# Wider margins for the state-loop products, the merging steps and the chunk-map steps of a hybrid decoder layer

## The chip, the cores and the metric

One core of a Trainium2 chip runs the kernel. The metric is the device time of one execution in microseconds (us); lower is better. The times below are the runs of the kernel before and one profiled execution of it.

## The reference

One decoder layer on 512 tokens of width 2048, all in float32: RMSNorm, one input projection, three groups of heads, a gate, an output projection and the residual. Cut to what matters here:

```python
h = _rms(x, norm_g)
proj = h @ w_in                                   # (512, 2048) @ (2048, 7296)
pa, pb, pc = _split(proj, (A_COLS, B_COLS, C_COLS))
r, k, v, ga, wd, ad = _split(_token_shift(pa, mu_a), ...)
ya = _rwkv7(r, k, v, wd, ad, ...) * silu(ga)      # 12 heads of 64: the delta rule
yb = _pool(pu, pool_w, pool_scale) * silu(pg)     # trailing means
yc = _stick_breaking(qc, kc, vc, ...) * silu(gc)  # 12 heads of causal attention
x = x + concatenate([ya, yb, yc]) @ w_out

# _rwkv7, for each token of each head:
sa = einsum('vk,k->v', state, -kk_t)
state = state * w_t + outer(sa, kk_t * a_t) + outer(v_t, k_t)
y_t = einsum('vk,k->v', state, r_t)
```

## The kernel before, in words

**The projections.** The input projection is cut into 57 tiles of 128 columns. Three of them are computed at the start, the other 54 one after the other (`project`, line 482). A tile takes 16 blocks of 128 rows in two half tiles of 8 blocks; each block takes three matmuls of 512 columns (`three`, line 454), because each operand is held as a rounded high part and a low rest (`hh`, `hl`; `wh`, `wl`). So a half tile is 24 matmuls. Its 512 KB of weights come by a transfer on SP's queue into `raw`; ScalarE makes `wh`, VectorE makes `wl` (`split_weights`, line 445), one half tile ahead. The output projection (`oacc`, from line 1074) follows in the same manner, in four column blocks; the first block goes through the 16 row blocks of y in the list `Y_ORDER`, 12 matmuls for each. In that list the last pair of the delta rule stands at place 14 (from 0).

**The delta rule** (`rwkv`, line 554) runs for six pairs of heads, each as a chunked form with 8 chunks of 64 tokens. For a pair: products for decay and rates; products between keys in a chunk (`gm`, into `lt`, `amr`, `bx`); transfers out and back; an inversion of 32 x 32 blocks as 30 dependent pairs of VectorE operations (`pr`, `xblk`); transfers back into `lt`; then the **merging** of the blocks (`xt`, 32 matmuls `q1` from line 710, a copy `w1`, 32 matmuls `q2` from line 720); the **chunk maps** (16 matmuls `am` from line 736, copied by ScalarE to `amx`, then in two halves 16 matmuls `gh` each from line 744, which VectorE adds into `bx`); and the **state loop** (line 776): for each of 8 chunks one product `s` with the state, whose two halves VectorE scales into the next chunk's place in `uv`, and one product `y`. At the end the output is normalised (`mu`, `var`, line 796 on) and gated (`y<-yc,y`, line 810).

**What may start when.** A pair's first work waits until the inversion of the pair before is done (line 557), and its `bk` and `amr` until the pair before has its chunk maps (`done[("mid", p)]`, line 753). Its state loop waits for the state loop before.

**Who sets the order.** Side work (delta rule, attention, pooling) is written as generators. After each matmul of a projection `pump` (line 417) lets every generator go on whose time has come. That time is worked out while the program is written, from a clock `pace` that adds up assumed costs of matmuls and of the other engines' operations (lines 98 to 190). A generator yields a function made by `need` or `need2`: the assumed time at which its inputs are ready and a PSUM bank is free, plus a margin. So the margin says how many matmuls of the projection are written into TensorE's order ahead of the step; on the chip TensorE takes its instructions in that order and waits if the inputs are late. The general margin `MARGIN` is 2.5; two shorter ones serve the delta rule's serial parts:

```python
def need(*tiles, tag=None, margin=MARGIN):                                   # line 388
        return margin + (max(t, pace.bank_at(tag, BANKS[tag])) if tag else t)

yield need(xt, tag="g", margin=QUICK)                                        # line 707, merging, ahead of q1
yield need(w1, tag="g", margin=QUICK)                                        # line 718, merging, ahead of q2
yield need(lt, amt, tag="c", margin=QUICK)                                   # line 734, am, two halves
yield need2(amx, bx, tag="c", margin=QUICK)                                  # line 742, gh, two halves
yield need(bx, uv, tag="y" if cc % 4 == 0 else None if last else "c", margin=TIGHT)   # line 778, each of 8 chunks
```

If an output-projection row block is asked for and its generator is not through, `load_y` (line 1039) pumps all generators at once, without matmuls between (`pump(True)`). VectorE's evictions of `q1`, `q2`, `gh` and `s` stand in blocks `with urgent()`, which move them forward in their engine's order.

Of the kernel before, what the change touches and what calls it, by code (L numbers as in the profile page):

```python
# [51 lines left out]
NFIRST = 3  # L52
BANKS = {"pj": 2, "g": 3, "c": 2, "y": 1}
MARGIN = 2.5
TIGHT = 0.8
AHEAD = 300
EVACUATE = 25
DL = 4.0
QUICK = 1.0
SCAN = 150  # L60
TP = 16

# [155 lines left out]
def hybrid_trunk_kernel(ctx: ExitStack, tc: tile.TileContext, x, xT, w_in, w_out, vecs, consts, up_w, pool_w, out):  # L218
# [41 lines left out]
    def gb(s="g"):  # L260
        return bank("g", s)

    def cb(s="c"):
        return bank("c", s)
# [123 lines left out]
    def need(*tiles, tag=None, margin=MARGIN):  # L388
        def at():
            t = max([pace.ready.get(Pace.key(a), 0.0) for a in tiles] + [0.0])  # L390
            return margin + (max(t, pace.bank_at(tag, BANKS[tag])) if tag else t)

        return at

    def need2(*tiles, tag="g", margin=MARGIN):
        def at():
            q = pace.slots.get(tag, [])
            t = max([pace.ready.get(Pace.key(a), 0.0) for a in tiles] + [0.0])
            free = sorted([pace.read.get(k, 1e9) for k in q] + [0.0] * (BANKS[tag] - len(q)))
            return margin + max(t, free[1])  # L400

        return at
# [151 lines left out]
    def rwkv(p):  # L554
# [149 lines left out]
        with urgent():  # L704
            for h in range(2):
                dve.transpose(xt3[h * HD:h * HD + B], lt[h * HD:h * HD + B, :, h, 0:B])
        yield need(xt, tag="g", margin=QUICK)
        q1 = gb("q1")
# [5 lines left out]
        with urgent():  # L714
            for h in range(2):
                r0 = h * HD + B
                dve.tensor_copy(out=w1[r0:r0 + B, :], in_=q1[r0:r0 + B, :NC_ * B])
        yield need(w1, tag="g", margin=QUICK)
        q2 = gb("q2")
# [13 lines left out]
        for half in range(2):  # L733
            yield need(lt, amt, tag="c", margin=QUICK)
            g = cb("am")
# [4 lines left out]
        for half in range(2):  # L740
            cs = slice(4 * half, 4 * half + 4)
            yield need2(amx, bx, tag="c", margin=QUICK)
            gs = [cb("gh"), cb("gh")]
# [32 lines left out]
        for cc in range(NC_):  # L776
            last = cc + 1 == NC_
            yield need(bx, uv, tag="y" if cc % 4 == 0 else None if last else "c", margin=TIGHT)
            if not last:
# [384 lines left out]
```

## Time and profile before

| | us |
|---|---|
| runs of the kernel, median (lowest to highest, 3 runs) | 1031.54 (1031.24 to 1035.27) |
| the profiled execution's own time | 1034.42 |
| its span in the profile | 1032.6 |

| engine | busy us | share of the span | instructions |
|---|---|---|---|
| TensorE matmul (PE) | 989.5 | 96% | 5132 |
| TensorE weight load (PEld) | 791.3 | 77% | 5132 |
| VectorE (DVE) | 660.9 | 64% | 1249 |
| ScalarE (ACT) | 512.0 | 50% | 838 |
| GpSimd (POOL) | 151.8 | 15% | 204 |

In the rows, a start is in us from the start of the span. "128*128 128x512" is a matmul's stationary and moving operand. Matmuls overlap: a row may say 0.39 us where the next one starts 0.23 us later. What stands in square brackets, or after the second bar of a group, is idle time of the engine just before, with what ended it. Line L380 is the helper of all matmuls, L212 of all work on the other engines, so groups are told apart by their tiles: `s<-uv,bx` writes `s` and reads `uv` and `bx`. The tiles `q1` and `q2` stand there as `q`.

### The profile page before, as it was taken

The page shows a single profiled execution, that of the slowest core. Times are in us where ns is not written, and L with a number is a line of the kernel's source. Part 1 is how long each engine was busy: PE and PEld are TensorE (multiplying, and loading weights), DVE is VectorE, ACT ScalarE, POOL GpSimd, SP SyncE. Part 2 cuts the span into 40 slices and gives each one's busy share as a digit, 9 for nine tenths or more (in the row PEclk, how much of TensorE's full clock was granted, in tenths as well). Part 3 has the DMA queues.
Part 4 walks back from the last instruction along what each step waited for, and adds up shares of the span by engine and source line. Part 5 has one row for each costly group of instructions (what it writes and reads, how often), then busy time and mean ns, then how long its engine had stood idle before and what let it go on. Part 6 is the DMA issues. An engine that isn't in the chain of part 4 may idle for free.

```text
span 1032.6 us, 13786 instructions
## 1 busy us (share of the span) xinstructions
PE 989.5 (96%) x5132; PEld 791.3 (77%) x5132; DVE 660.9 (64%) x1249; ACT 512.0 (50%) x838; POOL 151.8 (15%) x204
## 2 busy tenths in 40 slices
PE   8999989899899999999998998999999999999998
PEld 7868876787677786778777776777877888888886
DVE  5369674868749686697857778478884666323132
ACT  5656654656456555647546464355663345122211
POOL 0122211021211212102110021111221111000000
PEclk9999999999999999999999999999999999999999
DMA  9522232122221323113231222312232237724241
GB/s 340 199 87 84 90 93 97 52 77 97 88 82 62 90 83 109 71 61 95 84 117 43 86 68 96 103 59 76 92 95 95 74 136 257 262 88 139 102 143 61
DMA packets 62211, 109.18 MB, mean 106 GB/s; under 512 B 29760, under 2 KB 31168, under 8 KB 62144
## 3 DMA queue, kind: packets, MB, share of 16 engines
q1 hardware_dynamic: 62144, 108.30, 31.3%
q8 instruction: 40, 0.66, 0.3%
q14 instruction: 27, 0.22, 0.1%
HBM read 98.84 MB, written 9.44 MB: 105 GB/s over the span
## 4 chain that ended last, share of the span: by engine, by line
PE 39%; DVE 29%; issue 15%; ACT 8%; POOL 5%; DMA 2%; SPq 0%; POOLq 0%; DVEq 0%
PE oacc L380 17%; PE pj L380 16%; DVE wl L212 5%; DVE xblk L212 3%; DVE pr L212 3%; DVE n L212 3%; DVE bx L212 3%; POOL e L212 2%; ACT e L212 2%; PE first L380 2%; ACT n L212 2%; DVE u L212 1%; DVE amr L212 1%; DVE w L212 1%; ACT wh L212 1%
## 5 line engine op out<-in xcount | busy, mean ns | idle before, releaser
L380 PE MATMUL pj<-hh,wl 128*128 128x512 f32 x864 | 346.2, 401 | 14.0 <-DVE wl L212 14.0
L380 PE MATMUL pj<-hh,wh 128*128 128x512 f32 x864 | 345.8, 400 | 2.6 <-ACT wh L212 2.4
L380 PE MATMUL pj<-hl,wh 128*128 128x512 f32 x864 | 346.1, 401 | 0.0
L212 DVE TENSOR_TENSOR wl<-raw,wh 128x1024 fp32r<-128x1024 f32 x140 | 175.9, 1257 | 158.4 <-ACT wh L212 157.9
L212 ACT CAST wh<-raw 128x1024 fp32r<-128x1024 f32 x140 | 146.5, 1047 | 201.3 <-PE oacc L380 118.0
L380 PEld LDWEIGHTS pj<-hh,wl 128*128 128x128 f32 x864 | 163.9, 190 | 53.8 <-DVE wl L212 20.1
L380 PEld LDWEIGHTS pj<-hh,wh 128*128 128x128 f32 x864 | 163.9, 190 | 37.4 <-ACT wh L212 4.1
L380 PEld LDWEIGHTS pj<-hl,wh 128*128 128x128 f32 x864 | 164.0, 190 | 34.5 <-issue 2.2
L380 PE MATMUL oacc<-wl,yh 128*128 128x512 f32 x256 | 100.0, 391 | 0.0
L380 PE MATMUL oacc<-wh,yh 128*128 128x512 f32 x256 | 99.6, 389 | 0.0
L380 PE MATMUL oacc<-wh,yl 128*128 128x512 f32 x256 | 99.6, 389 | 0.0
L212 POOL TENSOR_SCALAR e<-e 128x512 f32<-128x512 f32 x28 | 45.0, 1607 | 200.1 <-ACT e L212 183.9
L212 DVE TENSOR_TENSOR_SCAN n<-n,m 128x512 f32<-128x512 f32 (+3 forms) x48 | 40.9, 866 | 32.7 <-ACT n L212 32.7
L212 POOL TENSOR_TENSOR d<-u 128x512 f32<-128x512 f32 x25 | 39.4, 1577 | 146.9 <-DVE u L212 90.1
L380 PEld LDWEIGHTS oacc<-wh,yl 128*128 128x128 f32 x256 | 48.0, 188 | 10.1 <-issue 0.2
L380 PEld LDWEIGHTS oacc<-wl,yh 128*128 128x128 f32 x256 | 48.0, 188 | 10.1 <-issue 0.2
L380 PEld LDWEIGHTS oacc<-wh,yh 128*128 128x128 f32 x256 | 48.0, 188 | 10.1
L212 ACT ACTIVATE e<-e 128x512 f32<-128x512 f32 x50 | 31.5, 630 | 33.4 <-POOL e L212 33.1
L212 DVE TENSOR_TENSOR u<-pj,rstd 128x512 f32<-128x512 f32 x50 | 34.3, 686 | 20.9 <-PE pj L380 20.6
L212 POOL CAST kl<-klo 64x512 fp32r<-64x512 f32 x24 | 20.9, 869 | 168.9 <-DVE klo L212 124.1
L212 DVE TENSOR_TENSOR pr<-xblk,nblk 128x60 f32<-128x60 f32 (+8 forms) x180 | 42.1, 234 | 4.7
L212 DVE TENSOR_TENSOR xblk<-xblk,pr 128x60 f32<-128x60 f32 (+8 forms) x180 | 41.1, 228 | 4.8
(203 smaller groups left out, 1240.2 us busy)
## 6 DMA issues: line engine op xcount, KB each, us to landing
raw<-in_w_in SPq DMA_DIRECT2D x108, 512.0 KB, 3.4
raw<-in_w_out SPq DMA_DIRECT2D x32, 512.0 KB, 3.5
lt<-in_x SPq DMA_DIRECT2D x8, 512.0 KB, 3.9
xr<-in_x SPq DMA_DIRECT2D x16, 256.0 KB, 5.9
out<-xr SPq DMA_DIRECT2D x16, 256.0 KB, 3.4
yin<-yd SPq DMA_DIRECT2D x14, 256.0 KB, 4.8
fr<-in_w_in SPq DMA_DIRECT2D x12, 256.0 KB, 7.1
nblk<-s SPq DMA_DIRECT2D x24, 128.0 KB, 3.4
```

Of the source, the lines that this page charges most:

```text
L212: return call(*args, **kw)
L380: pe.matmul(o, lhsT, rhs, start=start, stop=stop)
```

## The change

Two constants are made larger. `TIGHT`, the margin ahead of each chunk of the state loop, goes from 0.8 to 2.0; `QUICK`, the margin ahead of the merging steps and of the two kinds of products of the chunk maps, from 1.0 to 1.8. Nothing else is edited: the operations, their operands and the buffers are the same, and what can differ is where in each engine's order they stand.

```diff
 MARGIN = 2.5
-TIGHT = 0.8
+TIGHT = 2.0
 AHEAD = 300
 EVACUATE = 25
 DL = 4.0
-QUICK = 1.0
+QUICK = 1.8
 SCAN = 150
```

## Rows read from the trace of the kernel before

**Rows 1.** The page, part 1: busy us, share of the span, instructions of each engine.

```profile
PE 989.5 (96%) x5132; PEld 791.3 (77%) x5132; DVE 660.9 (64%) x1249; ACT 512.0 (50%) x838; POOL 151.8 (15%) x204
```

**Rows 2.** The waits of PE in the whole span: total, times, longest (us).

```profile
PE pj L380 <- DVE wl L212: 14.0, 14, 2.1
PE s L380 <- DVE uv L212: 6.9, 7, 2.6
PE gh L380 <- DVE bx L212: 3.5, 5, 1.3
...
PE y L380 <- DVE uv L212: 1.3, 1, 1.3
...
PE s L380 <- ACT kr L212: 1.0, 1, 1.0
...
PE s L380 <- DVE bx L212: 1.0, 1, 1.0
```

**Rows 3.** Timeline of PE, first pair's state loop: start, us, operation, idle before.

```profile
202.40 0.39 PE L380 MATMUL pj<-hh,wh 128*128 128x512 f32 x1
205.38 0.46 PE L380 MATMUL s<-uv,bx 128*128 128x128 f32 x2 [2.59 <-DVE uv L212]
...
207.84 1.16 PE L380 MATMUL gm<-amr,bk 64*128 64x128 f32 x16
...
209.27 0.38 PE L380 MATMUL s<-uv,bx 128*128 128x128 f32 x2
...
212.04 0.38 PE L380 MATMUL s<-uv,bx 128*128 128x128 f32 x2
```

**Rows 4.** Timeline of DVE in the same stretch.

```profile
199.61 0.69 DVE L212 TENSOR_TENSOR bx<-gh,amr 64x512 f32<-64x512 f32 x1
...
201.53 0.69 DVE L212 TENSOR_TENSOR amr<-d,E 128x512 f32<-128x512 f32 x1
...
203.52 1.22 DVE L212 TENSOR_TENSOR wl<-raw,wh 128x1024 fp32r<-128x1024 f32 x1
204.65 0.58 DVE L212 TENSOR_SCALAR uv<-s,ec 64x64 f32<-64x64 f32 x2
```

**Rows 5.** Timeline of PE, four more places where a moved step waits.

```profile
336.21 0.46 PE L380 MATMUL s<-uv,bx 128*128 128x128 f32 x2 [1.35 <-DVE uv L212]
...
351.73 0.49 PE L380 MATMUL y<-bx,uv 128*128 128x128 f32 x2 [1.25 <-DVE uv L212]
...
686.44 0.46 PE L380 MATMUL gh<-bx,amx 64*128 64x128 f32 x2 [1.35 <-DVE bx L212]
687.74 1.33 PE L380 MATMUL gh<-bx,amx 64*128 64x128 f32 x14 [0.85 <-DVE bx L212]
```

**Rows 6.** Windows: stretch, length, busy us (instructions) by engine, granted clock, DMA.

```profile
688.50:691.90 3.40, 3.40 (x15) 2.79 (x12) 3.37 (x6) 3.19 (x8) 0.00 (x0) 0.50 0.03 7
```

**Rows 7.** Windows, first state loop, the stretch behind it, the second pair's inversion.

```profile
199.00:225.00 26.00, 23.41 (x143) 19.25 (x142) 21.61 (x43) 11.98 (x19) 4.42 (x5) 1.00 0.28 81
225.00:241.00 16.00, 16.00 (x78) 13.37 (x77) 9.01 (x14) 13.10 (x24) 1.73 (x8) 1.00 0.23 66
241.00:272.00 31.00, 25.82 (x116) 20.24 (x116) 28.22 (x81) 16.01 (x29) 7.62 (x11) 1.00 0.20 73
```

**Rows 8.** The waits of PE between 241 and 272 us.

```profile
PE pj L380 <- DVE wl L212: 5.2, 4, 2.1
```

**Rows 9.** The waits of SP's queue: total, times, longest (us).

```profile
SPq L226 <- DVE wl L212: 600.8, 110, 13.6
SPq L226 <- DVE xblk L212: 69.9, 13, 9.3
```

**Rows 10.** Tile views: count, ns least/median/most, first and last start (us).

```profile
L380 PE MATMUL s<-uv,bx x84: 270/273/422, 199.9 to 823.5; 128*128 128x128 f32 x84
...
L212 DVE TENSOR_TENSOR y<-yc,y x6: 676/683/686, 252.1 to 847.8; 128x512 f32<-128x512 f32 x6
...
L380 PE MATMUL var<-sh,bmean_r x6: 388/396/398, 242.4 to 840.3; 128*128 128x512 f32 x6
...
L380 PE MATMUL oacc<-wh,yh x256: 388/389/397, 853.7 to 1028.0; 128*128 128x512 f32 x128
```

**Rows 11.** Window: the stretch in which the output projection's first block runs.

```profile
854.00:892.00 38.00, 38.00 (x168) 31.08 (x167) 17.70 (x21) 15.20 (x21) 3.01 (x2) 1.00 0.80 280
```

## The prediction

> **What bounds the kernel now.** I read the busy times first, then TensorE's waits, then the timeline at the places that the change moves. TensorE is busy for 989.5 of 1032.6 us [rows 1]: its stream of matmuls is the kernel, and only the 43 us in which it stands idle can be won without removing work. The list of waits says who ends them [rows 2]. The largest group, 14.0 us, is projection matmuls that wait for `wl`; the change doesn't move those. The moved steps hold four lines that I add up: `s` for `uv` 6.9, `y` for `uv` 1.3, `s` for ScalarE 1.0 and for `bx` 1.0, together 10.2 us in ten waits in the state loops, and `gh` for `bx` 3.5 us in five.
>
> The timeline shows why a state step waits [rows 3, 4]. The second product `s` of the first pair starts 2.98 us after the last projection matmul ahead of it; 2.59 us of that is idle. VectorE works in its order, and the two halves of `uv` came only behind a `wl` of 1.22 us that began at 203.52. Two chunks later nothing waits: from 209.27 to 212.04 is 2.77 us, which is the place that the margin of 0.8 gives. So the margin suffices when VectorE is free, and falls short when something long stands ahead of the eviction.
>
> **The change, part by part.** It adds and removes no operation. Each chunk of a state loop is placed 1.2 us later after its inputs, which is 1.2 / 0.226 = 5 or 6 more projection matmuls ahead of it; the 0.226 us per matmul is 38.00 us over the 168 starts of a stretch without waits [rows 11]. Each merging or chunk-map step goes 0.8 us later: 3 or 4 matmuls. These matmuls have to run anyway; moving them ahead costs nothing as long as their weights are there.
>
> *State loops.* A wait shrinks by at most 1.2 us. Of the ten, only three are longer: 2.59, 1.35 and 1.25 [rows 3, 5], and they keep 1.39 + 0.15 + 0.05 = 1.6. So 10.2 - 1.6 = 8.6 us go. Bounds: nothing, if VectorE's evictions slip by as much as the products, to all 10.2, if they also move forward.
>
> *Chunk maps.* `gh` waits 3.5 us; the margin takes at most 0.8 from a burst. The largest burst waits twice, 1.35 and 0.85 [rows 5]; the second is behind the next eviction of 0.7 us and stays when only the first shrinks, so 1.4 of its 2.2 is left. The others are 1.3 in total, in three bursts, and almost all goes. I take 2.0; bounds 0 and 3.5. The merging steps and `am` show no wait in the list, so their move gains nothing.
>
> *Clock.* From inside that burst on the granted clock is 0.50, the 1.2 GHz level, for 3.4 us [rows 6]; at half clock this costs 1.7 us. In the state loop with the 2.59 us wait it stays at 1.00, the 2.4 GHz level [rows 7]. I count half of the one dip, 0.8; bounds 0 and 1.7. The Trainium skill (TensorE: Matmul & The Clock Gate, "A second HAM failure mode: psum-queue depth-cycling") says that frequent short idles between groups of matmuls make the clock swing between its levels; the rows agree at 688 us and not at 199 us. By that rule the whole dip would go with the waits, and the sum below would be 9.3 instead of 8.4.
>
> *What is late next.* VectorE does not get faster. In the first state loop it is busy 21.6 of 26 us, then 9.0 of 16, then 28.2 of 31 in the second pair's inversion [rows 7]. In that last stretch TensorE waits 5.2 us for `wl` [rows 8]. If VectorE had no idle time between, what TensorE saves in the loop would be waited for there. It has 7 us in the middle stretch, against about 2 us saved per pair, so most is kept. But other pairs have shorter gaps, and the inversion stretches end full. Bounds: nothing comes back, or all 10.6. I take 3.0, nearer to the low end, because of the 7 us.
>
> *What is moved with the steps.* Each pair's `gm`, its transfers and its inversion start from the chunk maps of the pair before: the last eviction of `gh` is at 199.61, `amr` is written at 201.53, `gm` follows at 207.84 [rows 3, 4]. So the delay adds up over the pairs. Five placements lie in that circle (`q1`, `q2`, `am`, and `gh` twice; the second `am` is placed with the first): 5 x 0.8 = 4.0 us a pair, 24 us for six, and the last state loop adds 8 x 1.2 = 9.6, together 33.6 us. With them move the pair's 16 small transfers (by the code) on SP's queue and GpSimd's memsets. SP's queue is in order, and it stands 69.9 us behind unfinished inversions while weights queue up [rows 9]; since it also waits 600.8 us for `wl` to free buffers, a transfer moved by 4 us changes which weights stand behind it, in either direction. I cost this at nothing and put 4 us each way into the range, a quarter of the 14.0 us of `wl` waits that it could reshuffle; no row gives it a sign.
>
> *The end.* The last pair's result is needed by the output projection at place 14, after 14 x 12 = 168 matmuls: 853.7 + 38.0 = 891.7 now [rows 10, 11]. It is written at 847.8 + 0.7 = 848.5 [rows 10]: 43 us of cover. After the change both move forward by the gain and the result moves back by 33.6, so some 8 us of cover are left when the split of the block into its two parts, about 1.4 us, is paid. `var`, now at 840.3, is then placed 20 us into the output projection, where VectorE and ScalarE are busy less than half of the time [rows 11]. Cost nothing, with little to spare.
>
> **Sum.** 8.6 + 2.0 + 0.8 - 3.0 = 8.4 us. The profiled execution took 1034.42 us, so 1026.0 for its like; the median of the runs is 2.9 us below it, and from that 1031.5 - 8.4 = **1023.1 us**.
>
> **The rivals.**
>
> *The waits come back at the inversions* (chance 0.25). For it: VectorE is 91% busy there and already late by 5.2 us [rows 7, 8]; five pairs have a successor whose inversion lies behind their loop. Against: the idle time between. If four fifths of the 10.6 return and the dip stays, the gain is 2 us: 1029.5.
>
> *The last pair comes too late* (chance 0.07, the slower side). The serial circle through the six pairs grows, and cover at the end runs out. For it: the delay is carried from pair to pair and only 8 us of 43 are left. Against: the sum of placements, 33.6, is a ceiling for the planned times. It decides when the delay exceeds 43 - 1.4 = 42 us. At 60 us, if steps fall behind other generators' bursts, the output projection stands 18 us, or the remaining steps are pumped out without cover: 18 - 8.4 is 10 us slower, 1041.
>
> *The change does nothing* (chance 0.03). A margin is added to the later of inputs and bank, so a step can't stay where it is except by rounding to a matmul, and 1.2 us is five of them. Only if the engines' final order undid it: 1031.5.
>
> The forecast holds the rest, 0.65.
>
> **How the numbers follow.** The best corner of the forecast is 8.6 + 2.0 + 1.7 with nothing returned, 12.3 us, and part of the reshuffle with it: 1017. The upper end takes in the rival of the inversions and no change at all: 1031.5. Left out are a larger luck below (about 0.06), the late last pair (0.07) and some of the reshuffle above (0.05). A measurement of this kernel tells about 0.5%, 5.2 us, from no change: faster means below 1026.4, slower above 1036.7. The forecast lies below that bound except for 0.03 of it, and a lucky reshuffle brings 0.02 from the rival of the inversions: faster 0.64. Most of that rival, no effect, and the rest: same 0.28. Slower: the late last pair and a bad reshuffle, 0.08.
>
> **What would show it.** Right: in the list of waits the four lines of `s` and `y` fall from 10.2 to about 2 us and `gh` from 3.5 to about 1.5; steps of the state loop follow each other after 3.9 us or more instead of 2.7; `wl` waits rise from 14.0 to some 17; the clock dip at 688 us is gone or halved; the last `var` starts some 25 us later, behind the first `oacc`, and no `oacc` waits in its first block. The rival of the inversions shows as `wl` waits of 22 us or more with `s` waits gone. The late last pair shows as an `oacc` that waits for `yh` or `yl` some 38 us into the output projection. I am wrong if `s` still waits 5 us or more, which would mean that VectorE's evictions move back with the products, or if waits of a kind that is not in the list now make up the gain.

## The result, and the profile after

The changed kernel takes 1010.67 us in the median (1009.92 to 1011.55, 4 runs), against 1032.86 for the kernel before on the same chip (1031.24 to 1035.27, 4 runs): a ratio of 0.9782, 95% interval 0.9766 to 0.9797. That is 22 us less, where the prediction had 8.4 and a range from 1017 to 1031.5. The profiled execution took 1011.55 us, its span 1009.8. Faster was right; the size was wrong by more than a factor of two.

The page of the changed kernel, busy us by engine, answers to [rows 1]:

```profile
PE 983.2 (97%) x5132; PEld 790.0 (78%) x5132; DVE 660.2 (65%) x1249; ACT 511.2 (51%) x838; POOL 146.2 (14%) x204
```

The instructions are as many as before. Of the 22.8 us by which the span fell, 16.5 are idle time of TensorE (1032.6 - 989.5 = 43.1, now 1009.8 - 983.2 = 26.6). The other 6.3 stand in its busy time. Its waits answer to [rows 2]; total, times, longest:

```profile
PE pj L380 <- DVE wl L212: 12.5, 9, 2.4
PE first L380 <- ACT first L212: 2.1, 1, 2.1
PE pj L380 <- ACT wh L212: 2.0, 1, 2.0
...
PE s L380 <- DVE uv L212: 1.1, 3, 0.4
...
PE s L380 <- ACT k L212: 0.3, 1, 0.3
PE s L380 <- ACT kr L212: 0.3, 1, 0.3
```

`s` and `y` wait 1.7 us instead of 10.2, `gh` and the next pair's `gm` no longer stand in the list (3.5 and 1.3 before), and `wl` waits fell from 14.0 to 12.5 instead of rising. Together `s`, `y`, `gh` and `gm` went from 15.0 to 1.7; I call them the loop's waits below.

The second pair's state loop in TensorE's timeline (start, length, operation, idle before) answers to [rows 3]:

```profile
323.60 0.38 PE L380 MATMUL s<-uv,bx 128*128 128x128 f32 x2
...
328.00 0.46 PE L380 MATMUL s<-uv,bx 128*128 128x128 f32 x2 [0.38 <-DVE uv L212]
...
331.57 1.16 PE L380 MATMUL gm<-amr,bk 64*128 64x128 f32 x16
333.00 0.38 PE L380 MATMUL s<-uv,bx 128*128 128x128 f32 x2
```

VectorE in the same stretch answers to [rows 4]:

```profile
316.26 0.69 DVE L212 TENSOR_TENSOR bx<-gh,amr 64x512 f32<-64x512 f32 x1
316.99 0.68 DVE L212 SCALAR_TENSOR_TENSOR bk<-c,e 64x512 f32<-64x512 f32 x1
...
318.90 0.69 DVE L212 TENSOR_TENSOR bk<-e,e 64x512 f32<-64x512 f32 x1
319.50 0.69 DVE L212 TENSOR_TENSOR amr<-sq,E 64x512 f32<-64x512 f32 x1
...
323.48 0.69 DVE L212 TENSOR_TENSOR bx<-gh,amr 64x512 f32<-64x512 f32 x1
...
326.07 0.68 DVE L212 TENSOR_TENSOR amr<-d,E 128x512 f32<-128x512 f32 x1
...
327.28 0.58 DVE L212 TENSOR_SCALAR uv<-s,ec 64x64 f32<-64x64 f32 x2
```

These are the rows to look at: of the next pair's `bk` and `amr` (four and two operations of half the partitions, 0.7 us each; the `amr` of 128 partitions at 326.07 is another), five are made between the evictions of the two halves of `gh`, and the sixth, an `amr`, still earlier, at 309.35. All six stand ahead of the last eviction at 323.48. Counted in VectorE's timeline for the five pairs that have a successor, the changed kernel has 6, 6, 6, 6 and 6 of these six ahead of the last `gh` eviction. The kernel before has 4, 5, 3, 0 and 1; the rest stood behind it, in the state loop, among the `uv` evictions. I call those that stand ahead the early operations. In the program, `bk` and `amr` are written only after both halves of `gh` (lines 606 and 753). That VectorE takes them sooner comes about when the final order of each engine is set, and no run here shows by what rule.

### The profile page after: what moved, and what is told of

Read it like the earlier page. It is cut to its first block, busy times and chain, and to the rows that moved or that the text cites. A ratio compares the mean times of both kernels' runs of the same rounds, so it can differ in the third digit from the quotient of the medians.

```text
span 1009.8 us, 13791 instructions
## 1 busy us (share of the span) xinstructions
PE 983.2 (97%) x5132; PEld 790.0 (78%) x5132; DVE 660.2 (65%) x1249; ACT 511.2 (51%) x838; POOL 146.2 (14%) x204
## 4 chain that ended last, share of the span: by engine, by line
PE 58%; DVE 24%; issue 9%; ACT 4%; POOL 3%; DMA 2%; SPq 0%; DVEq 0%; POOLq 0%
PE pj L380 30%; PE oacc L380 17%; DVE wl L212 4%; DVE xblk L212 3%; DVE pr L212 3%; DVE bx L212 3%; DVE u L212 2%; PE first L380 2%; DVE n L212 2%; PE gm L380 1%; DMA lt<-in_x 1%; PE o L380 1%; POOL e L212 1%; PE wT L384 1%; DVE bk L212 1%
## 5 line engine op out<-in xcount | busy, mean ns | idle before, releaser
L380 PE MATMUL pj<-hh,wl 128*128 128x512 f32 x864 | 345.1, 399 | 12.5 <-DVE wl L212 12.5
L212 ACT CAST wh<-raw 128x1024 fp32r<-128x1024 f32 x140 | 146.4, 1046 | 198.7 <-PE oacc L380 115.9
L380 PEld LDWEIGHTS pj<-hh,wl 128*128 128x128 f32 x864 | 164.0, 190 | 49.9 <-DVE wl L212 16.4
L212 POOL TENSOR_TENSOR d<-u 128x512 f32<-128x512 f32 x25 | 30.8, 1231 | 145.9 <-DVE u L212 64.3
L212 ACT ACTIVATE w<-w 128x512 f32<-128x512 f32 (+1 forms) x36 | 20.2, 560 | 48.4 <-DVE w L212 47.7
```

Of the source, the lines that this page charges most:

```text
L212: return call(*args, **kw)
L380: pe.matmul(o, lhsT, rhs, start=start, stop=stop)
```

## The experiments

Theory A: each margin takes away the waits of its own steps. It was the prediction's. Rivals formed on the way: B and C, the place of the pairs against the projection tiles; D, both margins have to be wide and work by their own width; E, what counts of the merging margin is that the chunk maps come behind the next pair's preparation. In the table, times are medians, ratios are to the kernel before with their intervals, waits are in us, summed from the lists, and "early" counts the early operations by pair.

| run | TIGHT, QUICK | us | ratio | s and y | gh | gm | wl and wh | early |
|---|---|---|---|---|---|---|---|---|
| before | 0.8, 1.0 | 1032.9 | | 10.2 | 3.5 | 1.3 | 16.4 | 4 5 3 0 1 |
| changed | 2.0, 1.8 | 1010.7 | 0.977 to 0.980 | 1.7 | 0 | 0 | 14.5 | 6 6 6 6 6 |
| e1 | 2.0, 1.0 | 1035.7 | 1.000 to 1.003 | 3.1 | 2.2 | 7.9 | 17.0 | 4 0 0 0 1 |
| e2 | 0.8, 1.8 | 1038.2 | 1.003 to 1.006 | 13.7 | 0.7 | 0 | 18.5 | 6 6 5 5 6 |
| e3 | 1.4, 1.4 | 1026.2 | 0.991 to 0.994 | 7.1 | 0.7 | 1.2 | 17.5 | 6 0 6 4 6 |
| e4 | 0.8, 1.0, xt later | 1033.4 | 0.998 to 1.001 | 5.5 | 2.5 | 2.6 | 17.5 | 0 1 2 1 2 |
| e5 | 2.2, 1.8 | 1015.1 | 0.979 to 0.984 | 0.7 | 0.9 | 0.9 | 15.8 | 6 2 6 6 6 |
| e6 | 2.0, 1.6 | 1014.1 | 0.979 to 0.984 | 1.9 | 0 | 0.9 | 16.1 | 6 6 6 6 6 |
| e7 | 0.8, 2.6 | 1030.0 | 0.995 to 0.998 | 14.6 | 0.9 | 0.9 | 3.5 | 6 6 6 6 6 |
| e8 | 1.4, 1.0 | 1046.1 | 1.008 to 1.015 | 7.5 | 2.0 | 2.1 | 21.9 | 4 0 0 0 0 |
| e9 | 2.0, only gh 1.8 | 1034.3 | 0.999 to 1.001 | 4.0 | 0.9 | 1.5 | 17.7 | 6 2 1 1 1 |
| e10 | 2.0, q1, q2, am 1.8 | 1029.0 | 0.994 to 0.998 | 3.9 | 3.2 | 0.9 | 18.8 | 6 1 5 5 6 |
| e11 | 2.0, only q1, 5.0 | 1022.8 | 0.986 to 0.991 | 2.1 | 1.6 | 1.0 | 16.0 | 6 0 6 6 5 |
| e12 | 2.4, 2.6 | 1006.4 | 0.970 to 0.974 | 3.5 | 0 | 0 | 2.5 | 6 6 6 6 6 |
| e13 | 2.0, 1.8, next pair late | 1027.8 | 0.993 to 0.996 | 1.9 | 0 | 4.7 | 18.4 | 2 2 2 2 2 |
| e14 | 2.0, 1.0, next pair early | 1026.1 | 0.991 to 0.995 | 1.1 | 0 | 0 | 17.0 | 6 6 4 6 6 |
| e15 | 2.4, 2.2 | 1013.9 | 0.980 to 0.983 | 5.5 | 0 | 1.5 | 6.4 | 6 6 6 6 6 |

**One margin at a time, half of both, and the chain moved alone.**

e1, `TIGHT` alone:

```diff
-TIGHT = 0.8
+TIGHT = 2.0
```

> TIGHT 2.0 with QUICK left at 1.0: only the state-loop products are placed later. Theory A (each margin takes away the waits of its own steps, and what goes beyond them is small): the 10.2 us of waits ahead of s and y fall to about 2, gh keeps about 3.5, time about 1032.9 - 9 = 1024. Theory B (some 9 us of the gain of 22 come from the delta rule's chain standing elsewhere against the projection tiles, since the merging and chunk-map steps are in the circle that is carried from pair to pair and the state loop is not): the same 1024 here, with everything beyond it in the other margin.

e2, `QUICK` alone:

```diff
-QUICK = 1.0
+QUICK = 1.8
```

> QUICK 1.8 with TIGHT left at 0.8: only merging and chunk maps are placed later. Theory A: gh's 3.5 us go, s and y keep about 10, time about 1029. Theory B: the starts of the pairs also settle at an even distance of 118 to 119 us and the waits of gm, qm and wT and the unlisted short ones go with that: about 1020, with s and y still waiting some 10 us.

e3, half way:

```diff
-TIGHT = 0.8
+TIGHT = 1.4
-QUICK = 1.0
+QUICK = 1.4
```

> Both margins half way, TIGHT 1.4 and QUICK 1.4. Theory A: a wait shrinks by 0.6 us in a state step and by 0.4 in a chunk-map step; of the listed 10.2 and 3.5 us some 5.5 and 1.5 go, and the time lies between, at about 1032.9 - 11 = 1022. Theory B: the time does not follow the margins in proportion; it is near 1011 if the pairs come at an even distance, and near 1027 if not.

e4, margins as before, and the merging's transposes later:

```diff
-        yield soon(lt)
+        yield need(lt, margin=2.5)
```

> Margins as before (0.8 and 1.0), but the first step of the merging (the transposes into xt) is planned 4.0 us later, which is what the five placements of the changed kernel add to the circle of a pair. Theory A: no wait of the moved steps is widened, so the time stays within 4 us of 1033. Theory B: the circle stands against the tiles as in the changed kernel, so about 9 us are gained: 1024, with s, y and gh waiting as before.

Both theories fell. Neither margin alone gains anything: e1 is no faster than the kernel before and e2 is 0.4% slower, yet both together give 2.2%. e3, half way, gained 0.7%, less than A had it and near B's figure for uneven pairs. e4 stayed at 1033, as A had it and B had not. Since the next pair is let go behind the same line, e4 also moves that pair's preparation, which mattered later. In e1 the waits of `s` did go; here are four lines of its list of waits:

```profile
PE gm L380 <- DVE amr L212: 6.4, 5, 2.1
PE pj L380 <- ACT wh L212: 5.7, 5, 2.0
PE s L380 <- DVE uv L212: 3.1, 2, 2.3
...
PE gm L380 <- DVE bx L212: 1.5, 2, 1.0
```

They turned up one place further on, at `gm`, which waits for `amr`. The timelines of VectorE and of TensorE around the second pair of e1 show how:

```profile
318.45 0.69 DVE L212 TENSOR_TENSOR bx<-gh,amr 64x512 f32<-64x512 f32 x1
...
320.37 0.68 DVE L212 SCALAR_TENSOR_TENSOR bk<-c,e 64x512 f32<-64x512 f32 x1
...
324.12 0.58 DVE L212 TENSOR_SCALAR uv<-s,ec 64x64 f32<-64x64 f32 x2
...
325.92 0.69 DVE L212 TENSOR_TENSOR amr<-d,E 128x512 f32<-128x512 f32 x1
```

```profile
326.66 1.16 PE L380 MATMUL gm<-amr,bk 64*128 64x128 f32 x16 [1.14 <-DVE amr L212]
```

Here no early operation of this pair comes before the last `gh` eviction; `bk` and `amr` mix with the `uv` evictions, and what the wider margin gives to `s`, `gm` takes. In e2 28 of the 30 operations are early, and yet `s` and `y` wait longer than before, 13.7 us: with the narrow margin, an eviction of `uv` that stands behind a long operation is late all the same, as in [rows 3, 4]. From the timelines of TensorE and VectorE of e2:

```profile
334.64 0.77 PE L380 MATMUL s<-uv,bx 128*128 128x128 f32 x2 [2.81 <-DVE uv L212]
```

```profile
332.37 1.52 DVE L212 TENSOR_TENSOR wl<-raw,wh 128x1024 fp32r<-128x1024 f32 x1
333.92 0.58 DVE L212 TENSOR_SCALAR uv<-s,ec 64x64 f32<-64x64 f32 x2
```

**Is it the place against the tiles?** In the changed kernel's written order the third to the fifth pair follow each other after exactly 384 projection matmuls, the eight tiles of a pair. Theory C made that the cause. The four kernels differ in the two constants alone:

```diff
-TIGHT = 0.8
-QUICK = 1.0
+TIGHT, QUICK = 2.2, 1.8    # e5
+TIGHT, QUICK = 2.0, 1.6    # e6
+TIGHT, QUICK = 0.8, 2.6    # e7
+TIGHT, QUICK = 1.4, 1.0    # e8
```

> TIGHT 2.2 and QUICK 1.8: every margin at least as wide as in the changed kernel, but in the written order the state loops of the six pairs come after 398, 378, 377, 373 and 380 projection matmuls, where those of the changed kernel come after 385, 384, 384, 384 and 383 (384 matmuls are the eight tiles of a pair). Theory C (the gain beyond the moved waits comes from every pair standing at the same place against the tiles): that part is lost, about 1025 to 1032. Theory D (both margins have to be wide, and that is enough): about 1011, as the changed kernel.

> TIGHT 2.0 and QUICK 1.6: the pairs come after 385, 384, 384, 384 and 379 matmuls, at the same place against the tiles as in the changed kernel. Theories C and D: 1011 within 4 us.

> TIGHT 0.8 as before and QUICK 2.6: the pairs come after 403, 384, 384, 384 and 382 matmuls, evenly, with the narrow margin in the state loops. Theory C: the even distance alone gives its part, some 12 us; the state loops keep about 10 us of waits: about 1021. Theory D: without the wide state-loop margin no gain, 1030 or more.

> TIGHT 1.4 and QUICK 1.0: the pairs come after 363, 382, 384, 384 and 383 matmuls, evenly, at another place against the tiles (40 matmuls earlier) than in the changed kernel. Theory C, if evenness is what counts: about 1018; if the place counts too, anywhere between 1015 and 1033, the same waits repeated in each pair. Theory D: 1027 or more.

Theory C fell: e5 has the pairs at uneven distances and takes 1015; e8 has them even and takes 1046, the slowest of all. An even distance only repeats whatever happens in one pair, good or bad. e8 has the fewest early operations, 4 in all. e5 and e6, 3 to 4 us above the 1011 of D, speak for both margins being wide; e7 shows that `QUICK` 2.6 without a wide `TIGHT` leaves 14.6 us at `s` and `y`.

**Which of the merging steps, or what they do to the next pair?** All have `TIGHT` 2.0, except the last, which widens both constants further:

```diff
-            yield need2(amx, bx, tag="c", margin=QUICK)
+            yield need2(amx, bx, tag="c", margin=1.8)     # e9, alone
-        yield need(xt, tag="g", margin=QUICK)
+        yield need(xt, tag="g", margin=1.8)               # e10, and the same for w1 and for lt, amt
+        yield need(xt, tag="g", margin=5.0)               # e11, alone
+TIGHT, QUICK = 2.4, 2.6                                   # e12
```

> TIGHT 2.0; of the steps under QUICK only the two gh placements get 1.8, the others keep 1.0. In the written order the first gh of a pair comes 36, 26, 18, 24 and 18 projection matmuls behind the next pair's first product (dec); in the changed kernel 44, 38, 38, 38 and 38. Theory E (what counts of QUICK is that the chunk maps come behind the next pair's preparation, so that VectorE has made that pair's bk and amr before it has the last evictions of gh, and not inside the state loop): the preparation is again too late in four of five pairs, 1028 to 1036. Theory D (each step's own margin counts, above all that of gh): 1015.

> TIGHT 2.0; q1, q2 and am get 1.8, gh keeps 1.0. The first gh comes 41, 15, 36, 33 and 33 matmuls behind the next pair's dec. Theory E: the preparation is in time in four of five pairs, so most of the gain is there, 1013 to 1020, with gh waiting 1 to 2 us. Theory D: gh waits as before and without its margin the gain is lost, 1028 or more.

> TIGHT 2.0; all of the delay in one place: q1 gets a margin of 5.0, q2, am and gh keep 1.0. The first gh comes 62, 24, 49, 37 and 29 matmuls behind the next pair's dec. Theory E: in time in three or four of five pairs, 1013 to 1021, though no step but q1 has a wider margin, and q1 waits for nothing even now. Theory D: as with the state-loop margin alone, 1030 to 1036.

> TIGHT 2.4 and QUICK 2.6: wider than the change. The first gh comes 63, 53, 53, 53 and 53 matmuls behind the next pair's dec. Theory E: the preparation is well ahead in every pair, s and y wait less than 1 us, and the waits for wl may fall as they did with QUICK 2.6 and TIGHT 0.8 (3.5 us): 1000 to 1008, below the changed kernel. Against it: o waited 9 us for ScalarE there, and the last pair ends later, in the output projection; if that decides, 1012 to 1020.

e9 went as E had it: wide margins on `gh` itself, but the chunk maps come too soon after the next pair's start, few early operations, no gain. e11 gains 1.2% though only `q1`, which waits for nothing, was placed later: nearer to E than to D, a little above E's range, with one pair of five late. e10 is a miss for E and came out as D had it: 23 of the 30 operations are early, as in e11, and it takes 1029. There `gh` waits 3.2 us and `wl` and `wh` 18.8, so the width of `gh` counts too. e12 beats both kernels: 1006.4 us, 2.8% below the kernel before and below the changed kernel, whose interval begins at 0.9766 where that of e12 ends at 0.9744. E's time came out; that `s` and `y` would wait less than 1 us did not (3.5). Its page and its three largest waits:

```profile
PE 982.2 (98%) x5132; PEld 787.2 (78%) x5132; DVE 662.2 (66%) x1249; ACT 512.3 (51%) x838; POOL 154.2 (15%) x204
```

```profile
PE wT L384 <- ACT w L212: 4.6, 4, 1.9
PE s L380 <- DVE uv L212: 3.5, 9, 0.7
PE pj L380 <- DVE wl L212: 2.5, 2, 1.6
```

**The early preparation taken away and given back.** e13 is the changed kernel with the next pair let go later; e14 is e1 with the next pair let go sooner; e15 lies between the changed kernel and e12.

```diff
@@ e13: TIGHT 2.0, QUICK 1.8
-        done[("inv", p)] = True                       # from behind soon(lt)
         yield need(w1, tag="g", margin=QUICK)
+        done[("inv", p)] = True
@@ e14: TIGHT 2.0, QUICK 1.0
+        done[("inv", p)] = True
         dma(out=s2r, in_=xblk)
...
-        done[("inv", p)] = True
@@ e15
+TIGHT, QUICK = 2.4, 2.2
```

> Both margins as in the changed kernel (2.0 and 1.8), but the next pair's preparation is let go only after q1 and the wait for w1 instead of after xt. The first gh then comes 5, 6, 1, 1 and 1 matmuls behind the next pair's dec, not 44 to 38, while the state loops stand within 18 matmuls of where they were. Theory E (VectorE has to have made the next pair's bk and amr before the state loop): they fall into the state loop again and gm waits for amr; 1024 to 1036. Theory D (the wide margins themselves): 1011 to 1015.

> TIGHT 2.0 and QUICK 1.0, as in the run that widened the state loop alone (1035.7), but the next pair's preparation is let go before the inversion's result is sent out, some 10 us sooner. The first gh comes 39, 38, 31, 52 and 52 matmuls behind the next pair's dec. Theory E: without any wider margin in the merging and the chunk maps most of the gain is there, 1010 to 1020. Theory D: about 1035, with gh and gm waiting.

> TIGHT 2.4 and QUICK 2.2, between the changed kernel and the widest run (2.4 and 2.6, 1006.4). The first gh comes 65, 42, 42, 42 and 42 matmuls behind the next pair's dec. Theory E: 1004 to 1012, since every pair's preparation is early; waits for wl tell whether the widest run's 2.5 us of them belong to the width or to its place against the tiles.

e13 gives up 17 of the 22 us with both margins wide: as E had it, and not D. Its `gm` waits again, as this line of its list of waits and one of TensorE's timeline say, and `bk` stands behind `uv` in VectorE's order:

```profile
PE gm L380 <- DVE amr L212: 4.7, 2, 2.4
```

```profile
334.92 2.08 PE L380 MATMUL gm<-amr,bk 64*128 64x128 f32 x16 [2.29 <-DVE amr L212]
```

```profile
328.98 0.58 DVE L212 TENSOR_SCALAR uv<-s,ec 64x64 f32<-64x64 f32 x2
329.59 0.68 DVE L212 TENSOR_TENSOR bk<-e,e 64x512 f32<-64x512 f32 x1
```

The span of e13 is 17.8 us longer than that of the changed kernel. Only 4.9 of this are the loop's waits; the rest lies elsewhere, some 3.9 us at the weights, 4.5 in other listed waits and 4.7 in TensorE's busy time (987.9). The edit also holds back the rest of the next pair's preparation, its products for decay and rates and what follows from them, so this run does not tell the six operations apart from that.

e14 takes the loop's waits from 13.2 us in e1 to 1.1, lower than in the changed kernel, with the merging margin as narrow as before. So the loop's waits need two things, a wide `TIGHT` and the next pair's early operations, and the second can be had without `QUICK`. The two are not always enough: e15 has both and 7.0 us of these waits. And e14 gained only 9.6 us over e1 in time, short of E's 1010 to 1020, because other side products now wait; from its list of waits:

```profile
PE pj L380 <- DVE wl L212: 16.0, 14, 1.7
PE wT L384 <- ACT w L212: 4.0, 4, 1.6
PE mu L380 <- DVE sl L212: 2.2, 1, 2.2
...
PE q L380 <- DVE w L212: 1.8, 4, 0.7
```

e15 took 1013.9, just above its range. Its weight waits, 6.4 us, lie between those with `QUICK` 1.8 and 2.6. In all, E's times came out in e9, e12 and e13, were missed by 2 us in e11 and e15, and by 9 and 6 us in e10 and e14. It names a part of the cause, not all of it.

## Why the prediction was right or wrong

*State loops* (8.6 us). The size came out, 10.2 - 1.7 = 8.5. The reason given for it, that a margin takes up to its own width off a wait, did not: with that margin alone (e1) 7.1 us left `s` and `y`, 6.6 came to `gm`, and nothing was gained. That the size agrees is in part luck.

*Chunk maps* (2.0 us). 3.5 went, all that was there. The cap of 0.8 us on a burst assumed that VectorE would be as late as before; nothing of the 1.4 us that it left to the largest burst was there.

*Clock* (0.8 us). Nothing: the dip at 688 us [rows 6] is gone, but between 100 us and the last few us there are four dips of 3.4 us in the changed kernel (from 265, 384, 620 and 739 us) as there were before (from 272, 579, 634 and 688 us). One stands behind a `wh` wait at 738, as this window of the changed kernel shows (length, busy by engine, granted clock 0.50, the 1.2 GHz level):

```profile
739.50:742.90 3.40, 3.25 (x8) 2.57 (x9) 3.40 (x10) 2.79 (x8) 0.51 (x2) 0.50 0.44 159
```

*What is late next* (minus 3.0 us). This step failed: it had the sign wrong. It looked for returning waits only at the weights, and they fell by 1.9 us (`wl` and `wh`, 16.4 to 14.5). The windows that answer to [rows 7] show VectorE about as busy in the loop and in the inversion as before, while TensorE stands idle 0.3 us in the first stretch instead of 2.6 (the windows lie at the same times; the first state loop now runs on to 233 us, into the second):

```profile
199.00:225.00 26.00, 25.73 (x147) 20.95 (x147) 21.87 (x41) 13.82 (x24) 5.40 (x5) 1.00 0.26 83
225.00:241.00 16.00, 16.00 (x86) 13.48 (x85) 11.23 (x23) 12.40 (x24) 4.25 (x9) 1.00 0.29 80
241.00:272.00 31.00, 28.07 (x118) 22.26 (x117) 29.34 (x80) 17.47 (x32) 3.70 (x7) 0.94 0.22 78
```

Where waits did come back (e1), the next to wait was not the weights but `gm`, which shares VectorE's queue with the loop.

*What is moved with the steps* (cost and gain nothing) is the step whose mechanism failed. It counted the chunk maps' delay as a burden carried from pair to pair, and saw an effect of either sign at the weights alone. What it left out is that the next pair's preparation is let go by the inversion, ahead of every step that `QUICK` moves. So the delay also pushes the chunk maps behind that preparation, and in VectorE's order 30 of 30 operations of `bk` and `amr` stand ahead of the last `gh` eviction instead of 13. With both margins kept and the preparation let go later (e13), 17 of the 22 us are lost. That this order carries the whole of it is not shown: the loop's waits hold 4.9 us of e13's loss.

*The end* cost nothing, as predicted. Answering to [rows 10]:

```profile
L212 DVE TENSOR_TENSOR y<-yc,y x6: 657/680/682, 268.5 to 851.2; 128x512 f32<-128x512 f32 x6
...
L380 PE MATMUL var<-sh,bmean_r x6: 392/394/398, 253.5 to 844.8; 128*128 128x512 f32 x6
...
L380 PE MATMUL oacc<-wh,yh x256: 389/389/398, 829.8 to 1005.1; 128*128 128x512 f32 x128
```

`var` runs 15 us into the output projection (predicted 20), the result is there at 851.9, 22 us after the first `oacc`, and 38 us are allowed; no `oacc` waits. The delay of 33.6 us was a ceiling, as the prediction said of it: the last `var` starts 4.5 us later than before, where some 25 were expected.

*The sum.* The predicted 8.4 us fall short of the 22.8 us of span by 14.4. Of these, 6.3 lie in TensorE's busy time, 4.9 at the weights (plus 1.9 instead of minus 3.0), 1.5 at `gh`, 1.3 at `gm` and 1.2 in other listed waits; against them stand 0.8 for the clock and 0.1 at `s` and `y`. So the prediction's first step failed as well, that only the 43 us in which TensorE stands idle can be won: the same instructions were busy 6.3 us less. Nearly half of that lies in the bursts of `gh` and `gm`. These groups of TensorE's instructions, before and then in the changed kernel, say it (busy us, mean ns of one, idle before):

```profile
L380 PE MATMUL gh<-bx,amx 64*128 64x128 f32 x192 | 16.1, 287 | 3.6 <-DVE bx L212 3.5
L380 PE MATMUL gm<-amr,bk 64*128 64x128 f32 x192 | 14.6, 285 | 1.3 <-DVE bx L212 1.3
```

```profile
L380 PE MATMUL gm<-amr,bk 64*128 64x128 f32 x192 | 13.9, 285 | 0.1
L380 PE MATMUL gh<-bx,amx 64*128 64x128 f32 x192 | 13.9, 285 | 0.0
```

Now every burst of 16 takes 1.16 us, and twelve of them 13.9. Before, the burst that was broken at 686 us was busy for 0.46 and 1.33 us besides its waits, its end at the half clock [rows 5, 6]. `gh` and `gm` together hold 2.9 of the 6.3 us; I have not traced the other 3.4.

*The rivals.* The return at the inversions did not happen, the late last pair did not, and the change did what it says.

*Open.* The spread that the loop's waits don't explain: e14 and the changed kernel have 1.1 and 1.7 us of them and lie 15 us apart. Waits of `wl`, `wT`, `mu` and `qm` make up most of the difference in idle time, and why they are few with one arrangement and many with another was not settled; nor why the weight waits are only 2.5 to 6.4 us with `QUICK` 2.2 and 2.6.

## What to carry to other kernels

A list of waits on one engine is not a list of separate prices. Where several waits come from one engine's queue, giving one of them room can move it to the next consumer of that queue (e1); ask which instructions stand in that queue ahead of the late one, and whether they could be done sooner. When a serial step is placed later, look at what else is let go before it: most of the gain here was lost when the work that the delay allowed to slip in front was held back (e13). And try two placement constants together, not only one by one: each alone read as worthless, both together were worth 2.2%, and wider still 2.8%.

## What the runs showed that I had not expected

Two constants that only place the same 5132 matmuls move this kernel between 1006.4 and 1046.1 us, four per cent. A half-way setting of both gains 0.7%, while wider state-loop margins alone, at `TIGHT` 1.4 (e8), lose 1.1%.

How long TensorE waited does not by itself say whether the clock falls. In the changed kernel the granted clock fell to 0.50 behind single waits for weights of 1.84 to 2.43 us, but not behind one of 1.84 at 502 us. Before, it fell behind a `gm` wait of 1.26 us at 578 us and stayed at 1.00 in the state loop with a wait of 2.59 us [rows 3, 7]. Less idle time did not mean fewer dips there: 26.6 us instead of 43.1, and four dips in the middle of the kernel in both. Here are the waits at 502 us of the changed kernel and at 578 us of the kernel before, each with the window behind it:

```profile
501.99 0.50 PE L380 MATMUL pj<-hh,wl 128*128 128x512 f32 x1 [1.84 <-DVE wl L212]
502.00:505.40 3.40, 3.40 (x17) 2.82 (x18) 3.40 (x6) 1.72 (x5) 0.09 (x1) 1.00 0.42 154
```

```profile
577.88 0.57 PE L380 MATMUL gm<-amr,bk 64*128 64x128 f32 x5 [1.26 <-DVE bx L212]
579.30:582.70 3.40, 3.40 (x14) 3.01 (x13) 3.26 (x10) 0.59 (x1) 1.21 (x2) 0.50 0.12 21
```
